# Seven half-size products in one line, read from a shifted x

## The chip, the cores and the metric

The kernel runs on one core of one Trainium2 chip. The metric is the device time of one execution in microseconds (us). Three runs of the kernel before stand beside one profiled execution, from which all other times are taken.

## The reference

One sequence of 512 tokens with 1024 features passes two layers. Layer 0 mixes by a gated delta rule (six heads, chunked) beside a cross-attention into 256 memory tokens; layer 1 by sliding-window attention (12 query heads on a shared K/V, window 128, sinks) beside the same kind of cross-attention. Each mixer and each MLP is followed by `h = layer_norm(alpha * h + y)`. What the change concerns is the MLP, once in each layer:

```python
def sq_relu_mlp(h, w_up, w_down):            # w_up (1024, 4096), w_down (4096, 1024)
    return jnp.square(jax.nn.relu(h @ w_up)) @ w_down
```

All is float32.

## The kernel before, in words

**Split operands.** A float32 operand is kept as two tiles, a high part (h, hi, H) and the rest (l, lo, L). A product is three matmuls for each block of 128 features: high by high, high by low, low by high. The high part is made by a cast on ScalarE (ACT), the rest by a subtraction on VectorE (DVE): `wload` (L87, L88) for weights used as loaded, `split_copy` (L118, L119) elsewhere. The features of all tokens lie in XH and XL, [128, 8, 512] each.

**The MLP (`mlp`, L775).** The 4096 hidden features are eight chunks of 512. The first chunk (`ups_first`, 256 tokens at a time) and half of the second (`ups_second`) are made by plain products. All others go in pairs of 128-feature groups, two pairs to a chunk, by a Strassen-like scheme: for a pair, the 2 x 2 blocks (two groups, two halves of the tokens, two halves of the 1024 features) need seven half-size products instead of eight. `x_sums` (L831) makes three combinations of the blocks of x once in a layer (TH and TL, T2 to T4). `up_load` (L852) loads a pair's weights and makes four combinations on GpSimd (POOL), sa and sb; `Pair.split0`, `split_b`, `split_a` and `split2` make high and low parts of raw[0], sb, sa and half of raw[1] (w2h, w2l).

A product (`product`, L863) is twelve matmuls of 256 columns: four feature blocks, three matmuls each. The seven are

- m1 (A11 on x's block B11), into PSUM tile a; ACT copies it to s1. m2 (A12 on B21) adds onto a; ACT takes the relu of it into r.
- m6 (S2 on T2), into PSUM tile b; DVE makes u2 = s1 + b. m7 (S3 on T3) adds onto b; DVE makes u3 = s1 + b (L915) and, from it and d, a quarter of r (L916). m4 (A22 on T4) adds onto b again; DVE makes another quarter (L924).
- m5 (S1 on T1), into PSUM tile d. m3 (S4 on B22) adds onto d; DVE makes the last quarter (L928).

`close` (L930) squares r and splits it into hh and hl of the chunk being made ("later").

**The order.** The loop of L972 goes over seven chunks c and two halves n of the output features. One step is: the products m1, m6, m2, m5 and m7 of a pair of chunk c + 1; the first down tile of chunk c (`down`, L936: twelve matmuls of 512 columns for 128 tokens, added to the residual res by DVE); m4; the second down tile; m3 and `close`; the third and the fourth down tile. Between these calls stand the loads and splits of the down weights (`dn_slabs`) and of the next pair (`Pair`, `split0`, `split_b`, `split_a`). The first step of a layer has `ups_second` in place of a pair. A step with a pair is called a line in what follows.

The order in each engine's queue is fixed when the program is built. A scheduler places an instruction when its model finds its inputs ready, so the order may differ from that of the source: the cast of the next pair's first weights stands right behind m2's last use of the same buffer, two products ahead of where the source has it. Where an instruction of TensorE (PE) wasn't ready in the model, others were put ahead of it.

Weights are double: `wh` and `wl` have five buffers each, two for the down weights of a step and three for the splits of the next pair. Loads go through one queue (SP) into four buffers `wr`.

**Placement.** Pools lay their tiles one behind the other in the order of the first request for each tag, each tile rounded up to 32 bytes. In the program the start addresses within a partition, modulo 256 bytes, are: XH, XL and res 128; TH, TL, w2h and w2l 160; in the MLPs and in layer 1 wh and wl, and hh and hl, 224. Layer 1's attention features (mixh, mixl) are at 160. Blocks and halves within these tiles are 256 bytes or a multiple of it apart, so every slice that a product reads has its tile's value.

Of the kernel before, what the change touches and what calls it, by code (L numbers as in the profile page):

```python
# [11 lines left out]
F32 = mybir.dt.float32  # L12
F32R = mybir.dt.float32r
I32 = mybir.dt.int32
AF = mybir.ActivationFunctionType
ALU = mybir.AluOpType
AX = mybir.AxisListType

P = 128
S = 512  # L20
D = 1024
NT = S // P
# [27 lines left out]
def trunk(ctx: ExitStack, tc: tile.TileContext, xT, xn, memT, wk, wq, wv, wqm, wz, wmk, wmv, wo0, wo1, up, dn,  # L50
          bw, ws, conv, alog, dtb, nw, sinks, lng, lnb, lngb, pos, invf, out):
    nc = tc.nc
    V, G, A, T, SY = nc.vector, nc.gpsimd, nc.scalar, nc.tensor, nc.sync
# [8 lines left out]
    def nm(s):  # L62
        uid[0] += 1
        return f"{s}_{uid[0]}"

    def ct(shape, tag, dt=F32):
        return cp.tile(shape, dt, tag=tag, name=tag)

    def mmt(n="mm"):
        return pmm.tile([P, 512], F32, tag="mm", name=nm(n))  # L70
# [4 lines left out]
    def fr(ap):  # L75
        return ap.bitcast(F32)
# [4 lines left out]
    def wload(src, shape):  # L81
        wp = wpool[0]
        raw = wp.tile(shape, F32, tag="wr", name=nm("wr"), bufs=wpool[1])
        SY.dma_start(raw, src)
        hi = wp.tile(shape, F32R, tag="wh", name=nm("wh"), bufs=wpool[2])
        lo = wp.tile(shape, F32R, tag="wl", name=nm("wl"), bufs=wpool[2])
        A.copy(hi, raw)  # L87
        V.tensor_sub(lo, raw, fr(hi))  # L88
        return hi, lo

    XH = ct([P, KT, S], "XH", F32R)
    XL = ct([P, KT, S], "XL", F32R)
    res = ct([P, NT, D], "res")
    lns = ctx.enter_context(tc.tile_pool(name="lns", bufs=2))
    wa_stack = ExitStack()
    wpool[0] = wa_stack.enter_context(tc.tile_pool(name="wa", bufs=3))
# [20 lines left out]
    def split_copy(src, hi, lo):  # L117
        A.copy(hi, src)  # L118
        V.tensor_sub(lo, src, fr(hi))  # L119
# [8 lines left out]
    def tok(t):  # L128
        return slice(t * P, (t + 1) * P)
# [11 lines left out]
    def c0(shape, tag, dt=F32):  # L141

        return km0.tile(shape, dt, tag=tag, name=tag)
# [3 lines left out]
    ones = c0([P, P], "ones")  # L147
# [1 line left out]
    triu = c0([P, P], "triu")  # L149
    G.affine_select(triu, ones, [[1, P]], ALU.is_ge, 0.0, base=0, channel_multiplier=-1)  # L150
    slow = c0([P, P], "slow", F32R)
    slow32 = c0([P, P], "slow32")
    G.affine_select(slow32, ones, [[-1, P]], ALU.is_gt, 0.0, base=0, channel_multiplier=1)
    V.tensor_copy(slow, slow32)
    mtri = c0([P, P], "mtri")
    G.memset(mtri, 0.0)
    G.affine_select(mtri, mtri, [[1, P]], ALU.is_ge, NEG, base=0, channel_multiplier=-1)
    band = ct([P, 256], "band")
# [8 lines left out]
    convw = ct([P, 18, 4], "convw")  # L167
    gbT = ct([P, 4, 2, KT], "gbT")

    def row_bcast(src, n, tag):  # L170
        t = ct([P, n], tag)
        SY.dma_start(t, src.rearrange("(o n) -> o n", o=1).broadcast_to([P, n]))
        return t

# [22 lines left out]
    for i in range(2):  # L197
# [5 lines left out]
        for m in range(2):  # L203
            ps = mmt("VM")
            token_major(ps[:, :256], slabs, lambda k: MH[:, m, k, :], lambda k: ML[:, m, k, :])
            A.copy(VM[i][:, m, :], ps[:, :256])
        for j in range(2):
            w = wload(wmk[i, j], [P, KT, P])
            ps = mmt("KM")
            feature_major(ps[:, :256], w, lambda k: MH[:, :, k, :], lambda k: ML[:, :, k, :])  # L210
            A.copy(KM[i][:, j, :], ps[:, :256])
    for t in range(NT):
        split_load(xT[t], XH[:, :, tok(t)], XL[:, :, tok(t)])
    SY.dma_start(convw, conv)
    SY.dma_start(gbT, lngb)
    alog_b = row_bcast(alog, NH, "alog_b")
    dtb_b = row_bcast(dtb, NH, "dtb_b")
    nw_b = row_bcast(nw, P, "nw_b")
    sink_b = row_bcast(sinks, 12, "sink_b")
    invf_b = row_bcast(invf, 32, "invf_b")  # L220
    pos_i = ct([P, NT], "pos_i", I32)
# [11 lines left out]
    def proj_z(zg, gates=None):  # L233
# [4 lines left out]
        for t in range(NT):  # L238
            ps = mmt("proj_zMM")
            token_major(ps[:, :CW], slabs, x_tok(XH, t), x_tok(XL, t))  # L240
            A.copy(res[:, t, c0:c0 + n], ps[:, :n])
            if gates is not None:
                V.tensor_copy(gates[:, :, t], ps[:, n:n + 12])

    ab = ct([P, 12, NT], "ab")
    proj_z(2, ab)


    gg = [ct([P, 24], f"gate{i}") for i in range(12)]
    (ga, gb_, ge, gs, gs2, gacc, g_, beta, eg, neg, egl, gt) = gg  # L250

    def v6(t):
# [19 lines left out]
    for n in (13, 11, 9, 7, 5, 3, 1):  # L272
# [6 lines left out]
    A.activation(ea, alog_b, AF.Exp)  # L279
    V.scalar_tensor_tensor(v6(g_), v6(ga), -1.0, ea[:, :].unsqueeze(2).broadcast_to([P, NH, NT]),  # L280
                           op0=ALU.mult, op1=ALU.mult)
    gsp = [ct([P, 24], f"gsplit{i}", F32R) for i in range(2)]
    split_copy(g_, *gsp)
    ps = smt("v6ps")
    T.matmul(ps[:, 0:24], triu, g_, start=True, stop=True)
# [42 lines left out]
    def group_kq(gi, hl):  # L328
# [5 lines left out]
        for which, (wsrc, chb) in enumerate(((wk, 6), (wq, 0))):  # L334
            ps = mmt("kq")
            feature_major(ps, wload(wsrc[h], [P, KT, P]), x_all(XH), x_all(XL))
            conv_silu(ps, chb + h, kq[:, hl, :, which, :])
# [33 lines left out]
    def group_v(gi, hl):  # L371
        g = groups[gi]
        h = GH * gi + hl
        ps = mmt("v")
        feature_major(ps, wload(wv[h], [P, KT, P]), x_all(XH), x_all(XL))
        g["vt", hl] = dt_([P, 4, P], "vt")
# [221 lines left out]
    def features_half(src, t, j):  # L598

        pt = smt("to_feapt").rearrange("p (a i) -> p a i", a=4)  # L600
        for a in range(4):
            T.transpose(pt[:, a, :], src[:, (4 * j + a) * P:(4 * j + a + 1) * P], ident)
        hs, ls = XH[:, 4 * j:4 * j + 4, tok(t)], XL[:, 4 * j:4 * j + 4, tok(t)]
        A.copy(hs, pt)
# [14 lines left out]
    def proj_qm(j):  # L619
        ps = mmt("qm")  # L620
        feature_major(ps, wload(wqm[j], [P, KT, P]), x_all(XH), x_all(XL))
        A.copy(res[:, :, 768 + j * P:768 + (j + 1) * P], ps.rearrange("p (t i) -> p t i", t=NT))
# [152 lines left out]
    def mlp(pool, layer, last, gb0):  # L775
        NC = 8
        HT = 256
        kA, kB = slice(0, 4), slice(4, 8)
        tA, tB = slice(0, HT), slice(HT, S)
# [17 lines left out]
        def new_hid():  # L797
            return hid_tiles(F32R)
# [30 lines left out]
        xq = {}  # L829

        def x_sums():  # L831
            q = lambda k, t: (XH[:, k, t], XL[:, k, t])
            x11, x12, x21, x22 = q(kA, tA), q(kA, tB), q(kB, tA), q(kB, tB)
            t1 = f4([P, 4, HT], "t1")
            if layer == 0:
                f11, f12, f21, f22 = (xf[j][:, :, t] for j in range(2) for t in (tA, tB))
            else:
                f11, f12, f21, f22 = t1, *(f4([P, 4, HT], n) for n in ("f12", "f21", "f22"))
                for f, x in ((f11, x11), (f12, x12), (f22, x22), (f21, x21)):
                    V.tensor_tensor(f, fr(x[0]), fr(x[1]), op=ALU.add)  # L840
            V.tensor_sub(t1, f12, f11)
            V.tensor_sub(f12, f22, f12)
            V.tensor_sub(f22, f22, t1)
            V.tensor_sub(f21, f21, f22)
            TH, TL = (pool.tile([P, 3, 4, HT], F32R, tag=n, name=nm(n), bufs=1) for n in ("TH", "TL"))
            for i, t in enumerate((f22, f12, f21)):
                split_copy(t, TH[:, i], TL[:, i])

            xq.update(t1=t1, B11=x11, B21=x21, B22=x22, T1=x12,
                      **{n: (TH[:, i], TL[:, i]) for i, n in enumerate(("T2", "T3", "T4"))})  # L850
# [9 lines left out]
            G.tensor_tensor(sb[:, 1], raw[0][:, kB], sb[:, 0], op=ALU.subtract)  # L860
            return raw, sa, sb

        def product(ps, w, x, start, stop):  # L863
            (hi, lo), (mh, ml) = w, x
            for k in range(4):
                T.matmul(ps, hi[:, k, :], mh[:, k, :], start=start and k == 0, stop=False, skip_group_check=True)  # L866
                T.matmul(ps, hi[:, k, :], ml[:, k, :], start=False, stop=False, skip_group_check=True)  # L867
                T.matmul(ps, lo[:, k, :], mh[:, k, :], start=False, stop=stop and k == 3, skip_group_check=True)  # L868

        class Pair:  # L870
# [23 lines left out]

            def m1(self):
                self.a = smt("upa")[:, 0:HT]
                product(self.a, self.A11, xq["B11"], True, False)
                self.s1 = self.small("m1")
                A.copy(self.s1, self.a)

# [11 lines left out]
            def m7(self):  # L912
                product(self.b, self.S3, xq["T3"], False, False)
                self.u3 = self.small("u3")
                V.tensor_tensor(self.u3, self.s1, self.b, op=ALU.add)  # L915
                V.tensor_tensor(self.r[:, 1, tB], self.u3, self.d, op=ALU.add)  # L916

            def m5(self):
                self.d = smt("upd")[:, 0:HT]
                product(self.d, self.S1, xq["T1"], True, False)  # L920

            def m4(self):
                product(self.b, self.A22, xq["T4"], False, True)
# [48 lines left out]
        for c in range(NC - 1):  # L972
            later = new_hid()
            for n in range(2):
                p, nxt = nxt, None
                first = c == 0 and n == 0
                f0 = 4 * c + 2 * n + 6
                if first:
                    ups_second(later)
                    slabs = dn_slabs(c, n)  # L980
                else:
                    p.m1()
                    p.m6()
                    p.split2()
                    slabs = dn_slabs(c, n)
                    p.m2()
                    p.m5()
                    p.m7()
                if layer == 0 and c == 0:
                    ln_affine(gb0, ALPHA, n)  # L990
                if f0 < 4 * NC:
                    nxt = Pair(f0)
                down(c, 0, n, hid, slabs)
                if not first:
                    p.m4()
                if nxt:
                    nxt.split0()
                down(c, 1, n, hid, slabs)
                if not first:
                    p.m3()  # L1000
                    p.close(later)
                if nxt:
                    nxt.split_b()
                down(c, 2, n, hid, slabs)
                if nxt:
                    nxt.split_a()
                down(c, 3, n, hid, slabs)
            if c == 0:
                gb1 = load_gb(2 * layer + 1)
            if c == 2 and layer == 0:  # L1010
                rotary_tables(pool)
            hid = later
# [262 lines left out]
```

## Time and profile before

| | |
|---|---|
| runs | 1190.02, 1191.41, 1192.32 us; median 1191.41 |
| profiled execution | 1191.65 us, of it span 1189.9 us |
| mean granted clock of TensorE | 0.991 |
| PE matmuls | 7512, busy 1158.1 us |
| PE weight loads | busy 1025.7 us |
| VectorE / ScalarE / GpSimd | busy 866.3 / 566.3 / 229.0 us |
| DMA | 114.17 MB, 96 GB/s over the span |

In rows of the timeline the first column is the start in us from the span's start, the second the duration, then the engine, the line of the kernel, the operation, what it writes and reads (`out<-in`, buffer numbers left out), its shapes and how many were merged. In brackets stands the idle time before it on its engine and what ended that. PEld is a weight load of PE, POOL is GpSimd. Records of matmuls overlap, since one begins to stream before the results of the one before have landed: the pace of PE is the difference of two starts, not the duration.

### The profile page before, as it was taken

What the parts mean: (1) busy time and instruction counts of PE and PEld (TensorE: products, weight loads), DVE (VectorE), ACT (ScalarE), POOL (GpSimd) and SP (SyncE); (2) the same over time, 40 slices, a digit from 0 to 9 for tenths busy, and PEclk for the clock granted to TensorE, in tenths of its full rate; (3) what the DMA queues carried; (4) which work ended last, traced back from release to release, by engine and by line L of the source; (5) the groups of instructions that cost most, each with busy time, mean ns of one, the idle gap of its engine ahead of it and who ended that gap; (6) DMA issues with size and microseconds to landing.
All of it is one profiled execution on the core that took longest, in us unless ns stands there. A gap on an engine that the chain in (4) does not pass through costs nothing.

```text
span 1189.9 us, 19072 instructions
## 1 busy us (share of the span) xinstructions
PE 1158.1 (97%) x7512; PEld 1025.7 (86%) x7512; DVE 866.3 (73%) x1621; ACT 566.3 (48%) x1024; POOL 229.0 (19%) x180
## 2 busy tenths in 40 slices
PE   9899999999999999999999999999999999999996
PEld 8877788879998898998988888788989998989985
DVE  5478889777798666666656968886986666666657
ACT  5345454655484443545443346662653534445341
POOL 0112111101014413232220100000042314232204
PEclk9899999999999999999999999999999999999998
DMA  7522141204324232232424231112333242323311
GB/s 255 176 72 78 60 132 39 67 19 139 130 82 139 79 121 93 90 123 71 141 73 124 72 120 41 38 35 71 107 112 119 74 139 72 128 86 101 112 36 71
DMA packets 41242, 114.17 MB, mean 96 GB/s; under 512 B 12160, under 2 KB 12544, under 8 KB 41152
## 3 DMA queue, kind: packets, MB, share of 16 engines
q1 hardware_dynamic: 40576, 112.04, 28.9%
q8 instruction: 59, 0.97, 0.3%
q10 hardware_dynamic: 576, 0.92, 0.2%
q14 instruction: 31, 0.25, 0.1%
HBM read 109.53 MB, written 3.41 MB: 95 GB/s over the span
## 4 chain that ended last, share of the span: by engine, by line
PE 81%; DVE 11%; ACT 3%; DMA 1%; POOL 1%; issue 1%; POOLq 0%; SPq 0%; ACTq 0%; DVEq 0%
PE dn L113 9%; PE dn L114 9%; PE dn L112 9%; PE upb L866 3%; PE upb L867 3%; PE upb L868 3%; PE wo L113 2%; PE wo L114 2%; PE wo L112 2%; PE upa L867 2%; PE upd L867 2%; PE upa L868 2%; PE upd L868 2%; PE upa L866 2%; PE upd L866 2%; PE up L103 2%
## 5 line engine op out<-in xcount | busy, mean ns | idle before, releaser
L114 PE MATMUL dn<-wh,hl 128*128 128x512 f32 x512 | 200.0, 391 | 0.0
L113 PE MATMUL dn<-wl,hh 128*128 128x512 f32 x512 | 200.0, 391 | 0.0
L112 PE MATMUL dn<-wh,hh 128*128 128x512 f32 x512 | 199.6, 390 | 0.0
L87 ACT CAST wh<-wr 128x1024 fp32r<-128x1024 f32 (+1 forms) x136 | 142.5, 1051 | 103.8 <-PE dn L114 24.8
L88 DVE TENSOR_TENSOR wl<-wr,wh 128x1024 fp32r<-128x1024 f32 (+1 forms) x136 | 166.4, 1225 | 34.1 <-ACT wh L87 31.7
L114 PEld LDWEIGHTS dn<-wh,hl 128*128 128x128 f32 x512 | 96.1, 188 | 20.3
L945 DVE TENSOR_TENSOR res<-res,dn 128x512 f32<-128x512 f32 x120 | 82.0, 683 | 40.7 <-PE dn L114 40.2
L112 PEld LDWEIGHTS dn<-wh,hh 128*128 128x128 f32 x512 | 96.4, 188 | 17.6
L113 PEld LDWEIGHTS dn<-wl,hh 128*128 128x128 f32 x512 | 96.1, 188 | 17.7
L857 POOL TENSOR_TENSOR sa<-wr 128x512 f32<-128x512 f32 x26 | 36.1, 1388 | 370.6 <-DMA wr<-in_up_dram 279.6
L651 POOL TENSOR_TENSOR rs<-rs,nhalf 128x1 f32<-128x1 f32 x16 | 13.3, 834 | 338.1 <-DVE rs L650 282.0
L119 DVE TENSOR_TENSOR wl<-wr,wh 128x1024 fp32r<-128x1024 f32 x26 | 34.1, 1310 | 43.5 <-ACT wh L118 43.5
L118 ACT CAST wh<-sa 128x1024 fp32r<-128x1024 f32 x26 | 27.3, 1050 | 76.6 <-PE upd L867 76.6
L867 PE MATMUL upa<-XL,wh 128*128 128x256 f32 x208 | 58.5, 281 | 0.0
L867 PE MATMUL upd<-XL,wh 128*128 128x256 f32 x208 | 58.5, 281 | 0.0
L868 PE MATMUL upa<-XH,wl 128*128 128x256 f32 x208 | 58.4, 281 | 0.0
L868 PE MATMUL upd<-XH,wl 128*128 128x256 f32 x208 | 58.3, 280 | 0.0
L866 PE MATMUL upa<-XH,wh 128*128 128x256 f32 x208 | 58.3, 280 | 0.0
L866 PE MATMUL upd<-XH,wh 128*128 128x256 f32 x208 | 58.2, 280 | 0.0
L866 PE MATMUL upb<-TH,wh 128*128 128x256 f32 x208 | 58.0, 279 | 0.0
L867 PE MATMUL upb<-TL,wh 128*128 128x256 f32 x208 | 57.8, 278 | 0.0
L868 PE MATMUL upb<-TH,wl 128*128 128x256 f32 x208 | 57.6, 277 | 0.0
(411 smaller groups left out, 3365.7 us busy)
## 6 DMA issues: line engine op xcount, KB each, us to landing
wr<-in_up_dram SPq DMA_DIRECT2D x64, 512.0 KB, 5.4
wr<-in_dn_dram SPq DMA_DIRECT2D x64, 512.0 KB, 4.6
wr<-in_wo_dram SPq DMA_DIRECT2D x16, 512.0 KB, 3.8
wr<-in_bw_dram SPq DMA_DIRECT2D x8, 512.0 KB, 4.3
wr<-in_wz_dram SPq DMA_DIRECT2D x6, 520.0 KB, 4.5
wr<-in_wk_dram SPq DMA_DIRECT2D x6, 512.0 KB, 3.7
wr<-in_wq_dram SPq DMA_DIRECT2D x6, 512.0 KB, 3.5
wr<-in_wv_dram SPq DMA_DIRECT2D x6, 512.0 KB, 3.7
```

Of the source, the lines that this page charges most:

```text
L87: A.copy(hi, raw)
L88: V.tensor_sub(lo, raw, fr(hi))
L112: T.matmul(ps, sh, hi[:, kk, :], start=(k == 0), stop=False)
L113: T.matmul(ps, sh, lo[:, kk, :], start=False, stop=False)
L114: T.matmul(ps, sl, hi[:, kk, :], start=False, stop=(k == nk - 1))
L118: A.copy(hi, src)
L119: V.tensor_sub(lo, src, fr(hi))
L857: G.tensor_tensor(sa[:, 0], raw[1][:, kA], raw[1][:, kB], op=ALU.add)
L866: T.matmul(ps, hi[:, k, :], mh[:, k, :], start=start and k == 0, stop=False, skip_group_check=True)
L867: T.matmul(ps, hi[:, k, :], ml[:, k, :], start=False, stop=False, skip_group_check=True)
L868: T.matmul(ps, lo[:, k, :], mh[:, k, :], start=False, stop=stop and k == 3, skip_group_check=True)
L945: V.tensor_tensor(dst, dst, ps, op=ALU.add)
```

## The change

Three things change in the MLP. The seven products of a pair are called one after the other (m1, m6, m2, m7, m5, m4, m3), then `close`; the four down tiles follow without anything of the pair between them. m7 comes ahead of m5, and the quarter of r made from u3 and d moves from m7 to m5. And m1's first matmul of the twelve reads its moving block from a copy of it, made by ACT once in a layer.

The placement changes with it. 32 bytes ahead of XH put XH, XL and res at 160 modulo 256; 224 bytes behind res bring what follows back to where it was modulo 256. In the MLP's pool 64 and 160 bytes ahead of the copy put it at 128, 32 bytes before x's own 160, and 96 bytes behind it bring w2h and w2l to 224. For room, a mask's own tile (slow32) is dropped, its values going through mtri first, and small tiles of layer 0 (ab, the gates, gsplit, nw_b, 2048 bytes together) go to the pool that is closed with layer 0's mixer. No matmul is added or removed.

```diff
+    ct([P, 8], "pad0")
     XH = ct([P, KT, S], "XH", F32R)
     XL = ct([P, KT, S], "XL", F32R)
     res = ct([P, NT, D], "res")
+    ct([P, 56], "pad1")
...
-    slow32 = c0([P, P], "slow32")
-    G.affine_select(slow32, ones, [[-1, P]], ALU.is_gt, 0.0, base=0, channel_multiplier=1)
-    V.tensor_copy(slow, slow32)
     mtri = c0([P, P], "mtri")
+    G.affine_select(mtri, ones, [[-1, P]], ALU.is_gt, 0.0, base=0, channel_multiplier=1)
+    V.tensor_copy(slow, mtri)
     G.memset(mtri, 0.0)
...
-    ab = ct([P, 12, NT], "ab")
+    ab = c0([P, 12, NT], "ab")
...
             TH, TL = (pool.tile([P, 3, 4, HT], F32R, tag=n, name=nm(n), bufs=1) for n in ("TH", "TL"))
+            pool.tile([P, 16], F32, tag="pad2", name=nm("pad2"), bufs=1)
             for i, t in enumerate((f22, f12, f21)):
                 split_copy(t, TH[:, i], TL[:, i])
+
+            pool.tile([P, 40], F32, tag="pad3", name=nm("pad3"), bufs=1)
+            xq["first"] = pool.tile([P, HT], F32R, tag="x0", name=nm("x0"), bufs=1)
+            pool.tile([P, 24], F32, tag="pad4", name=nm("pad4"), bufs=1)
+            A.copy(xq["first"], fr(XH[:, 0, tA]))
...
-        def product(ps, w, x, start, stop):
+        def product(ps, w, x, start, stop, first=None):
             (hi, lo), (mh, ml) = w, x
             for k in range(4):
-                T.matmul(ps, hi[:, k, :], mh[:, k, :], start=start and k == 0, stop=False, skip_group_check=True)
+                m = mh[:, k, :] if k or first is None else first
+                T.matmul(ps, hi[:, k, :], m, start=start and k == 0, stop=False, skip_group_check=True)
                 T.matmul(ps, hi[:, k, :], ml[:, k, :], start=False, stop=False, skip_group_check=True)
                 T.matmul(ps, lo[:, k, :], mh[:, k, :], start=False, stop=stop and k == 3, skip_group_check=True)
...
-                product(self.a, self.A11, xq["B11"], True, False)
+                product(self.a, self.A11, xq["B11"], True, False, xq["first"])
...
                 V.tensor_tensor(self.u3, self.s1, self.b, op=ALU.add)
-                V.tensor_tensor(self.r[:, 1, tB], self.u3, self.d, op=ALU.add)
 
             def m5(self):
                 self.d = smt("upd")[:, 0:HT]
                 product(self.d, self.S1, xq["T1"], True, False)
+                V.tensor_tensor(self.r[:, 1, tB], self.u3, self.d, op=ALU.add)
...
                     p.m2()
+                    p.m7()
                     p.m5()
-                    p.m7()
+                    p.m4()
+                    p.m3()
+                    p.close(later)
...
                 down(c, 0, n, hid, slabs)
-                if not first:
-                    p.m4()
                 if nxt:
                     nxt.split0()
                 down(c, 1, n, hid, slabs)
-                if not first:
-                    p.m3()
-                    p.close(later)
```

More of the change, by code (lines that the diff above doesn't have):

```diff
@@ L168, in trunk, with row_bcast @@
     gbT = ct([P, 4, 2, KT], "gbT")
-    def row_bcast(src, n, tag):
-        t = ct([P, n], tag)
+    def row_bcast(src, n, tag, where=ct):
+        t = where([P, n], tag)
         SY.dma_start(t, src.rearrange("(o n) -> o n", o=1).broadcast_to([P, n]))
@@ L217, in trunk @@
     dtb_b = row_bcast(dtb, NH, "dtb_b")
-    nw_b = row_bcast(nw, P, "nw_b")
+    nw_b = row_bcast(nw, P, "nw_b", c0)
     sink_b = row_bcast(sinks, 12, "sink_b")
@@ L243, in proj_z @@
                 V.tensor_copy(gates[:, :, t], ps[:, n:n + 12])
-    ab = ct([P, 12, NT], "ab")
+    ab = c0([P, 12, NT], "ab")
     proj_z(2, ab)
-    gg = [ct([P, 24], f"gate{i}") for i in range(12)]
+    gg = [c0([P, 24], f"gate{i}") for i in range(12)]
     (ga, gb_, ge, gs, gs2, gacc, g_, beta, eg, neg, egl, gt) = gg
@@ L281, in trunk @@
                            op0=ALU.mult, op1=ALU.mult)
-    gsp = [ct([P, 24], f"gsplit{i}", F32R) for i in range(2)]
+    gsp = [c0([P, 24], f"gsplit{i}", F32R) for i in range(2)]
     split_copy(g_, *gsp)
```

## The prediction

> **What bounds the kernel now.** I read the page's busy times and chain first, then the timeline of TensorE (PE) over one step of an MLP, then ScalarE (ACT) and VectorE (DVE) over the same step.
>
> ```profile
> span 1189.9 us, 19072 instructions
> PE 1158.1 (97%) x7512; PEld 1025.7 (86%) x7512; DVE 866.3 (73%) x1621; ACT 566.3 (48%) x1024; POOL 229.0 (19%) x180
> PE 81%; DVE 11%; ACT 3%; DMA 1%; POOL 1%; issue 1%; POOLq 0%; SPq 0%; ACTq 0%; DVEq 0%
> ```
>
> PE is busy for 97% of the span and carries 81% of the chain. So a change pays only if it makes PE's instructions follow each other more closely, and it costs when PE has to wait. The span is 1189.9 us, the profiled execution 1191.65 us, and the median of the runs shown 1191.41 us, 0.24 us lower. I sum against 1191.65. About 0.2% (2.4 us) is what a measurement of this kernel can tell from no change.
>
> The next rows are the first matmuls of each product in one step (a "line" below): start in us, duration, operation. Only the starts matter, since matmuls overlap.
>
> ```profile
> 480.53 0.28 PE L866 MATMUL upa<-XH,wh 128*128 128x256 f32 x1
> ...
> 481.95 0.28 PE L866 MATMUL upb<-TH,wh 128*128 128x256 f32 x1
> ...
> 482.19 0.28 PE L868 MATMUL upb<-TH,wl 128*128 128x256 f32 x1
> ...
> 483.33 0.28 PE L866 MATMUL upa<-XH,wh 128*128 128x256 f32 x1
> ...
> 484.50 0.28 PE L867 MATMUL upa<-XL,wh 128*128 128x256 f32 x1
> ...
> 484.74 0.28 PE L866 MATMUL upd<-XH,wh 128*128 128x256 f32 x1
> ...
> 486.14 0.28 PE L866 MATMUL upb<-TH,wh 128*128 128x256 f32 x1
> ...
> 486.85 0.28 PE L866 MATMUL upb<-TH,wh 128*128 128x256 f32 x1
> ...
> 487.53 0.39 PE L112 MATMUL dn<-wh,hh 128*128 128x512 f32 x1
> ...
> 490.27 0.28 PE L866 MATMUL upb<-TH,w2h 128*128 128x256 f32 x1
> ...
> 491.70 0.39 PE L112 MATMUL dn<-wh,hh 128*128 128x512 f32 x1
> ...
> 494.46 0.28 PE L866 MATMUL upd<-XH,wh 128*128 128x256 f32 x1
> ...
> 495.89 0.39 PE L112 MATMUL dn<-wh,hh 128*128 128x512 f32 x1
> ...
> 498.62 0.39 PE L112 MATMUL dn<-wh,hh 128*128 128x512 f32 x1
> ...
> 501.34 0.28 PE L866 MATMUL upa<-XH,wh 128*128 128x256 f32 x1
> ...
> 503.01 0.28 PE L868 MATMUL upb<-TH,wl 128*128 128x256 f32 x1
> ...
> 504.14 0.28 PE L866 MATMUL upa<-XH,wh 128*128 128x256 f32 x1
> ```
>
> A line takes 501.34 - 480.53 = 20.81 us. Every product is twelve matmuls of one shape, yet they take, by differences of starts: m1 1.42, m6 1.38, m2 1.41, m5 1.40, m7 1.39, m4 (on w2h) 1.43 and m3 1.43, 9.86 us together; the four down tiles 2.74, 2.76, 2.73 and 2.72, 10.95 us. PE waits for nobody in there: the difference is pace. m6's last ten matmuls take 1.14 us (482.19 to 483.33) and, a line later, 1.13 (503.01 to 504.14): 113.5 ns each. m7 begins at 0.71/6 = 118 ns (486.14 to 486.85) and ends at 0.68/6 = 113.5. m1, m4 and m3 stay at 119.
>
> With the placements of the section on the kernel before, the 113.5 ns belong to a moving tile at 160 and weights at 224 (modulo 256 bytes), once something at 128 has been read just before; m1, m2, m5 and m3 move a tile at 128 over weights at 224, and m4 a tile at 160 over weights at 160, after a down tile. That is what the change builds on: it puts every operand of the seven products where m6 has them.
>
> **Part one, the line.** There are 13 lines in a layer (seven chunks with two halves, less the first), 26 in all. After the change the line is 84 matmuls on a moving tile at 160 and weights at 224, the first reading its copy at 128, as m6 is entered from m1. I take 113.5 ns: 84 x 0.1135 = 9.53 us, and 0.03 us for settling (m7's first six at 118 ns instead of 113.5). The down tiles are entered once instead of three times: 2.74 + 3 x 2.72 = 10.90. The line is then 20.46 us, 0.35 us less, and 26 of them 9.1 us less. From the other side, if the pace were that of m1 and m3 (1.43), the products would take 10.01 us and the line would be 0.10 us longer: +2.6 us.
>
> The rows say that the pace of one shape depends on what it reads. The Trainium skill, "TensorE: Matmul & The Clock Gate", section "Back-to-back issue gap", gives the gap at full clock as N/2.4 + 2.5 ns, which depends on the width alone (109 ns for 256, 216 for 512); by it this part, and the next but one, would be worth nothing. The trace disagrees: 113.5 and 119 ns stand side by side at one width.
>
> **Part two, a wait that the new order brings.** m7's sum leaves PSUM through u3 (L915), and m4 adds onto the same PSUM tile, so m4's first weight load must wait for u3. Now a down tile (2.74 us) lies between; afterwards only m5 does (1.36 us).
>
> ```profile
> 484.82 1.05 ACT L118 CAST wh<-wr 128x1024 fp32r<-128x1024 f32 x1 [2.29 <-PE upa L867]
> 485.90 1.22 DVE L119 TENSOR_TENSOR wl<-wr,wh 128x1024 fp32r<-128x1024 f32 x1 [1.88 <-ACT wh L118]
> 487.73 0.42 DVE L915 TENSOR_TENSOR u<-m,upb 128x256 f32<-128x256 f32 x1 [0.61 <-PE upb L868]
> ```
>
> As soon as m2's eleventh matmul (484.50) has given up the weights, ACT casts the next pair's into their buffer, and DVE takes the rest (wl) before u3. Counted from m2's end (484.74): cast at +0.08, wl from +1.16 to +2.38. u3's input will now be there one product and 0.20 us (487.53 to 487.73) after m2's end, at +1.56, while wl has held DVE since +1.16. So u3 runs from about +2.42 to +2.84, and m4 would be due at 2 x 1.362 = +2.72. That wl stays ahead of u3 in DVE's fixed order I take from a like case: at the end of the line wl of the down weights stands before the sum of the last down tile, though they are ready almost together (that tile's matmuls gave way to m1 at 480.53).
>
> ```profile
> 480.46 1.22 DVE L88 TENSOR_TENSOR wl<-wr,wh 128x1024 fp32r<-128x1024 f32 x1
> 481.60 0.68 DVE L945 TENSOR_TENSOR res<-res,dn 128x512 f32<-128x512 f32 x1
> ```
>
> What a wait for DVE costs beyond the delay:
>
> ```profile
> 777.11 0.68 DVE L119 TENSOR_TENSOR pTl<-spt,pTh 128x512 fp32r<-128x512 f32 x1
> ...
> 777.85 0.42 PEld L1145 LDWEIGHTS spt<-ident,pm 128*128 128x128 f32 x4 [0.56 <-DVE pTl L119]
> ```
>
> ```profile
> 682.19 0.19 PEld L112 LDWEIGHTS ropeMM<-wh,XH 128*128 128x128 f32 x1 [0.76 <-ACT vSh L118]
> ...
> 682.22 0.36 PE L112 MATMUL ropeMM<-wh,XH 128*128 128x256 f32 x1 [0.58 <-DVE rp L1043]
> ...
> 682.42 0.28 PE L113 MATMUL ropeMM<-wl,XH 128*128 128x256 f32 x1
> ```
>
> The weight load starts 0.06 us after DVE's end (777.79), the matmul 0.03 later, and the second matmul follows after 0.20 instead of 0.12 us. So m4 starts at +2.93, 0.21 late, and with 0.08 for the restart the wait costs 0.29 us. Behind it on PE's queue stand m4, m3 and all four down tiles: nothing hides it. It is paid where a next pair is cast, 12 lines of a layer, 24 in all: +7.0 us. The bounds are 0 (u3 goes first, or other matmuls fill the gap) and 0.29; I take 0.29, since its rows are of this very place. r's quarter (L916), which goes from m7 to m5, follows u3 at once and is ready long before m3 rewrites its tile.
>
> **Part three, other readers of x.** ups_first reads XH and XL as moving tiles over weights at 224, now at 128:
>
> ```profile
> 345.20 0.28 PE L103 MATMUL up<-XL,wh 128*128 128x256 f32 x1
> ...
> 354.33 0.39 PE L102 MATMUL up<-XH,wh 128*128 128x512 f32 x1
> ...
> 365.58 0.39 PE L112 MATMUL dn<-wh,hh 128*128 128x512 f32 x1
> ```
>
> From 345.20 to 354.33 there are 77 matmuls of 256 columns, 118.6 ns each; then 48 of 512 in 11.25 us, 234.4 ns each. With x at 160 the first become m6's case: 2 layers x 192 x (118.6 - 113.5) = 2.0 us less. No copy leads them in, so 0 is the other bound. For 512 columns at 160 over 224 there is no row; between no change and the down tiles' 2.72/12 = 226.7 ns (0.7 us over 96 matmuls) I take half, 0.4 us.
>
> In the projections x is the stationary side:
>
> ```profile
> 699.81 0.39 PE L112 MATMUL projqMM<-wh,XH 128*128 128x512 f32 x1
> ...
> 704.24 0.39 PE L113 MATMUL projqMM<-wl,XH 128*128 128x512 f32 x1
> ```
>
> 19 matmuls in 4.43 us, 233.2 ns. With x elsewhere they may fall to 226.7 or rise to 240 (twice the slowest 256-wide pace, 1.43/12 = 119, and a little): over the 288 such matmuls of layer 1, 1.9 us less or more. Layer 0's projections, on weights of several placements, I bound alike. I take 0 for these and keep 3 us either way for the range.
>
> **Parts that cost nothing.** The copy is one ACT instruction per layer, well before the first line, on an engine 48% busy. POOL's fill of mtri now waits for DVE's copy out of it, at the start, and nothing early reads what stands behind it on POOL. Tiles moved to the other pool keep their instructions. m4's and m3's sums reach DVE and ACT 2.7 to 7 us earlier than now, out of the down tiles' time; the hidden tile they make is first read a whole line later. SP's queue keeps its order of loads, and the sums on POOL wait for those as before.
>
> **Sum.** 1191.65 - 9.1 + 7.0 - 2.0 - 0.4 = 1187.2 us.
>
> **The rivals.**
>
> *The wait is covered (chance 0.31).* The pace comes as above, but u3 is done in time: it is put ahead of wl, or matmuls of the first down tile are put in front of m4. For it: where one operation wasn't ready, PE's order has others in between, as here a projection between transposes.
>
> ```profile
> 713.96 0.33 PE L1145 MATMUL spt<-ident,pm 128*128 128x128 f32 x1
> 714.04 0.48 PE L112 MATMUL projqMM<-wh,XH 128*128 128x512 f32 x1
> 714.36 0.93 PE L1145 MATMUL spt<-ident,pm 128*128 128x128 f32 x7
> ```
>
> One down matmul (0.227 us) would cover nearly all of it. Against it: in today's lines PE's order is that of the source, and the gap is so short that it may not have been seen when the order was made. Time: 1187.2 - 7.0 = 1180.2 us.
>
> *The pace is lost at the wait (0.16).* m4 and m3 restart without a copy leading them in and run as m4 and m3 do now, 1.43 instead of 1.36: 0.14 us x 26 = 3.5 us more, 1190.7 us.
>
> *Slower: the pace does not follow the placement (0.14).* What m6 has may come from the twelve matmuls at 128 before it, not from one; m7, entered alike, needed six matmuls to settle. Then the products keep their 9.86 us, the readers of part three gain nothing, only the down tiles' 0.05 us x 26 = 1.3 us remain, and the wait is paid: 1191.65 + 7.0 - 1.3 = 1197.4 us. It decides from a gain per line under 7.0/26 = 0.27 us, a mean pace above 114.4 ns (9.53 + 0.35 - 0.27 = 9.61 us over 84). The skill's rule on the gap, quoted above, has no term for placement and points the same way.
>
> **How the numbers follow.** My forecast, gain and wait together, gets 0.39. With 3 us of uncertainty from part three around it, about a quarter of it falls within 0.2%. The covered wait lies wholly on the fast side, the lost pace mostly within 0.2%, the last rival wholly on the slow side. Faster: 0.29 + 0.31 + 0.03 = 0.63; within: 0.09 + 0.11 = 0.20; slower: 0.01 + 0.02 + 0.14 = 0.17. The range goes from the covered wait less 2.7 us, 1177.5, to the lost pace and 3.3 us, 1194.0; the last rival is left out.
>
> **What would show it.** In the timeline of PE the 84 matmuls of a line should lie 113.5 ns apart from the second or third on, and a line should take about 20.75 us with the wait and 20.46 without. u3 behind wl and an idle weight load of m4 released by DVE would show the wait; a down matmul between m5 and m4 would show it covered. ups_first should go from 118.6 to 113.5 ns. It is wrong if m2 or m5 keep 117 ns, if m4 starts without a wait in unchanged order, or if projections change by more than 3 us.

## The result

| | before | after |
|---|---|---|
| median of four runs | 1191.87 us | 1185.35 us |
| lowest and highest | 1190.02 and 1192.34 | 1184.96 and 1185.52 |
| profiled execution, its span | 1191.65, 1189.9 us | 1185.52, 1183.8 us |
| mean granted clock of TensorE | 0.991 | 0.992 |

The ratio of the times is 0.9948, 95% interval 0.993 to 0.9965: the changed kernel is faster by 6.5 us, and its time lies 1.9 us below the forecast of 1187.2. These are the lines of the page after that answer to those of before:

```profile
span 1183.8 us, 19079 instructions
PE 1148.7 (97%) x7512; PEld 1017.0 (86%) x7512; DVE 864.5 (73%) x1621; ACT 563.4 (48%) x1026; POOL 247.9 (21%) x180
PE 82%; DVE 12%; ACT 3%; POOL 1%; issue 1%; DMA 1%; POOLq 0%; SPq 0%; ACTq 0%; DVEq 0%
```

PE still carries the chain, with the same 7512 matmuls, and is busy for 9.4 us less. One line of layer 0 in the timeline of PE, the first matmul of each product and of the down tiles (L875 to L877 are now what L866 to L868 were, L115 what L112 was):

```profile
498.99 0.28 PE L875 MATMUL upa<-x,wh 128*128 128x256 f32 x1
...
500.37 0.28 PE L875 MATMUL upb<-TH,wh 128*128 128x256 f32 x1
...
501.73 0.28 PE L875 MATMUL upa<-XH,wh 128*128 128x256 f32 x1
...
503.09 0.28 PE L875 MATMUL upb<-TH,wh 128*128 128x256 f32 x1
...
504.45 0.28 PE L875 MATMUL upd<-XH,wh 128*128 128x256 f32 x1
...
505.87 0.38 PE L875 MATMUL upb<-TH,w2h 128*128 128x256 f32 x1
...
507.34 0.28 PE L875 MATMUL upd<-XH,wh 128*128 128x256 f32 x1
...
508.70 0.39 PE L115 MATMUL dn<-wh,hh 128*128 128x512 f32 x1
...
519.60 0.28 PE L875 MATMUL upa<-x,wh 128*128 128x256 f32 x1
```

By differences of starts: m1 1.38, m6 1.36, m2 1.36, m7 1.36, m5 1.42, m4 1.47, m3 1.36, the four down tiles 10.90, the line 20.61 us where it was 20.81. Four products run at 1.36/12 = 113.3 ns a matmul; m1 takes 0.02 us longer to reach that pace. What m5 and m4 have above it is the wait for u3, at the end of the one and the start of the other.

Summed from the starts in the two traces, the 26 lines with their waits gained 3.6 us: 2.6 in layer 1, only 1.0 in layer 0. ups_first gained 0.9, the 512-wide matmuls behind it 0.1. The remaining 1.5 us lie outside the MLPs. Most of that is the start of the program, where the first matmul into kq comes 2.51 us earlier than before, and some is given back later. Here is that matmul, in the timeline before:

```profile
56.66 0.39 PE L102 MATMUL kq<-XH,wh 128*128 128x512 f32 x1
```

and after:

```profile
54.15 0.39 PE L105 MATMUL kq<-XH,wh 128*128 128x512 f32 x1
```

**What layer 0 lost.** In the first line of layer 0, m7 stands still (timeline after, several engines):

```profile
377.73 0.28 PE L877 MATMUL upa<-XH,wl 128*128 128x256 f32 x1
377.87 1.21 DVE L88 TENSOR_TENSOR wl<-wr,wh 128x1024 fp32r<-128x1024 f32 x1
...
379.00 0.41 DVE L914 TENSOR_TENSOR u<-m,upb 128x256 f32<-128x256 f32 x1
...
379.46 0.19 PEld L875 LDWEIGHTS upb<-TH,wh 128*128 128x128 f32 x1 [1.66 <-DVE u L914]
379.47 0.38 PE L875 MATMUL upb<-TH,wh 128*128 128x256 f32 x1 [1.46 <-DVE u L914]
```

DVE is behind with the splits of the down weights (wl, L88) and the residual sums of the first step, so u2 is finished at 379.41. m7 adds onto the PSUM tile that u2 reads, and m7 now stands directly behind m2, where m5 used to lie between. It starts 379.47 - 377.73 = 1.74 us after m2's last matmul instead of 0.11: 1.63 us, once in the program. Its second matmul follows 0.22 us later instead of 0.11, so the stall costs 1.7 us in all.

### The profile page after: what moved, and what is told of

Read it like the earlier page. It is cut to its first block, busy times and chain, and to the rows that moved or that the text cites. A ratio compares the mean times of both kernels' runs of the same rounds, so it can differ in the third digit from the quotient of the medians.

```text
span 1183.8 us, 19079 instructions
## 1 busy us (share of the span) xinstructions
PE 1148.7 (97%) x7512; PEld 1017.0 (86%) x7512; DVE 864.5 (73%) x1621; ACT 563.4 (48%) x1026; POOL 247.9 (21%) x180
## 4 chain that ended last, share of the span: by engine, by line
PE 82%; DVE 12%; ACT 3%; POOL 1%; issue 1%; DMA 1%; POOLq 0%; SPq 0%; ACTq 0%; DVEq 0%
PE dn L116 9%; PE dn L117 9%; PE dn L115 9%; PE upb L875 3%; PE upb L877 3%; PE upb L876 3%; PE wo L116 2%; PE wo L117 2%; PE wo L115 2%; PE upa L876 2%; PE upa L875 2%; PE upa L877 2%; PE upd L876 2%; PE upd L877 2%; PE upd L875 2%; PE up L106 2%
## 5 line engine op out<-in xcount | busy, mean ns | idle before, releaser
L88 DVE TENSOR_TENSOR wl<-wr,wh 128x1024 fp32r<-128x1024 f32 (+1 forms) x136 | 166.6, 1226 | 79.6 <-ACT wh L87 79.1
L115 PE MATMUL dn<-wh,hh 128*128 128x512 f32 x512 | 199.5, 390 | 0.0
L865 POOL TENSOR_TENSOR sa<-wr 128x512 f32<-128x512 f32 x26 | 44.2, 1702 | 349.0 <-DMA wr<-in_up_dram 294.8
L115 PEld LDWEIGHTS dn<-wh,hh 128*128 128x128 f32 x512 | 96.1, 188 | 19.0
L875 PE MATMUL upb<-TH,wh 128*128 128x256 f32 x208 | 57.5, 277 | 1.5 <-DVE u L914 1.5
L877 PE MATMUL upa<-XH,wl 128*128 128x256 f32 x208 | 57.5, 276 | 0.0
L877 PE MATMUL upb<-TH,wl 128*128 128x256 f32 x208 | 57.4, 276 | 0.0
L875 PE MATMUL upd<-XH,wh 128*128 128x256 f32 x208 | 57.4, 276 | 0.0
L877 PE MATMUL upd<-XH,wl 128*128 128x256 f32 x208 | 57.4, 276 | 0.0
L866 POOL TENSOR_TENSOR sb<-sa,wr 128x512 f32<-128x512 f32 x26 | 57.4, 2207 | 0.0
L121 ACT CAST wh<-wr 128x1024 fp32r<-128x1024 f32 x26 | 27.4, 1055 | 53.6 <-PE upa L876 53.6
```

Of the source, the lines that this page charges most:

```text
L115: T.matmul(ps, sh, hi[:, kk, :], start=(k == 0), stop=False)
L865: G.tensor_tensor(sa[:, 0], raw[1][:, kA], raw[1][:, kB], op=ALU.add)
L866: G.tensor_tensor(sb[:, 0], sa[:, 0], raw[0][:, kA], op=ALU.subtract)
L875: T.matmul(ps, hi[:, k, :], m, start=start and k == 0, stop=False, skip_group_check=True)
```

## The experiments

The kernels were timed on several occasions, so each has its ratio to the kernel before on the same chip, and the verdicts rest on the traces rather than on a microsecond of time. A handy sign there: in the view of groups by line the mean recorded length of a 256-column matmul goes with its pace, 281 ns where they follow each other every 117.7 ns, 276 where every 113.3. Three such groups before (columns: line, operation, count, busy us, mean ns, idle before):

```profile
L867 PE MATMUL upa<-XL,wh 128*128 128x256 f32 x208 | 58.5, 281 | 0.0
...
L868 PE MATMUL upd<-XH,wl 128*128 128x256 f32 x208 | 58.3, 280 | 0.0
...
L867 PE MATMUL upb<-TL,w2h 128*128 128x256 f32 x104 | 29.4, 283 | 0.0
```

and after:

```profile
L876 PE MATMUL upa<-XL,wh 128*128 128x256 f32 x208 | 57.7, 277 | 0.0
...
L877 PE MATMUL upd<-XH,wl 128*128 128x256 f32 x208 | 57.4, 276 | 0.0
...
L876 PE MATMUL upb<-TL,w2h 128*128 128x256 f32 x104 | 28.8, 276 | 0.0
```

"upa" is m1 and m2, "upd" m5 and m3, the rows on w2h are m4.

Two theories of the pace stand against each other. By the first it belongs to the placement: a matmul whose operands lie at 160 and 224 runs fast, whatever came before. By the second it belongs to the history: it is set where a run of matmuls begins, by a first read at 128 followed by reads at 160. A rival to both is that the gain comes from the new order.

### The copy left out (no_copy)

```
-                product(self.a, self.A11, xq["B11"], True, False, xq["first"])
+                product(self.a, self.A11, xq["B11"], True, False)
```

> The changed kernel, but m1's first matmul reads x's own block at 160 instead of the copy at 128 (the copy is still made). Theory P (placement alone draws the pace): a moving tile at 160 over weights at 224 settles at 113.5 ns whatever was read before, so a line grows by 0.03 us at most and the time stays within 1 us of the changed kernel's 1185.35. Theory H (entry): the pace is set by what is read when the line is entered, and then kept; coming from down tiles at 224 straight to 160 the products run at 117 to 120 ns like m4 before the change, 84 x 26 x 3.5 to 6.5 ns = 8 to 14 us more: 1193 to 1199.

1187.68 us (12 runs), ratio 0.9983 [0.9971, 0.9995]. The groups of this kernel:

```profile
L876 PE MATMUL upa<-XL,wh 128*128 128x256 f32 x208 | 58.4, 281 | 0.0
...
L877 PE MATMUL upd<-XH,wl 128*128 128x256 f32 x208 | 58.0, 279 | 0.0
```

One changed read in 84 slows m1, and then m6, m2, m7 and m5 with it, all to 1.41 us. So the pace is not each matmul's own, since m6's operands are untouched: it is handed on, and the placement theory falls. But upd stands between 276 and 281, because m3 runs at 1.36 in most lines: behind m4's wait the pace is fast again. The loss is smaller than the expectation's larger number, as the slow pace is 117.7 ns and not 119 to 120, and as the wait ends it.

### x back at 128, its copy at 96 (x_128)

```
-    ct([P, 8], "pad0")
-    ct([P, 56], "pad1")
-            pool.tile([P, 40], F32, tag="pad3", name=nm("pad3"), bufs=1)
+            pool.tile([P, 32], F32, tag="pad3", name=nm("pad3"), bufs=1)
-            pool.tile([P, 24], F32, tag="pad4", name=nm("pad4"), bufs=1)
+            pool.tile([P, 32], F32, tag="pad4", name=nm("pad4"), bufs=1)
```

> The changed kernel with x back at 128 modulo 256 and the copy 32 bytes before it, at 96; order and all else as changed. If placement sets the pace (P, and H as well, since x and TH then alternate between 128 and 160), m1, m2, m5 and m3 go back to 117 to 119 ns: 48 x 26 x 4 to 5.5 ns = 5 to 7 us more, and ups_first and the projections give back about 1 to 3 us: 1191 to 1195. If the one line alone had brought the gain, the time stays at 1185.4.

1191.18 us (11 runs), ratio 1.0007 [0.9997, 1.0017]. Groups of this kernel (its lines are two lower):

```profile
L875 PE MATMUL upd<-XH,wl 128*128 128x256 f32 x208 | 58.5, 281 | 0.0
L875 PE MATMUL upa<-XH,wl 128*128 128x256 f32 x208 | 58.3, 281 | 0.0
```

The new order and a copy 32 bytes below x, but with x at 128: no gain at all. In its timeline the first matmuls of m6, m2, m7 and m5 are

```profile
498.92 0.28 PE L873 MATMUL upb<-TH,wh 128*128 128x256 f32 x1
...
500.29 0.28 PE L873 MATMUL upa<-XH,wh 128*128 128x256 f32 x1
...
501.70 0.28 PE L873 MATMUL upb<-TH,wh 128*128 128x256 f32 x1
...
503.11 0.28 PE L873 MATMUL upd<-XH,wh 128*128 128x256 f32 x1
```

Here m6 alone, a step from 128 to 160, gets down to 1.37 us, and m2 behind it, back at 128, loses it again. But m7 behind m2 is the same step, and stays at 1.41. So a read at 128 ahead of reads at 160 doesn't always bring the fast pace; what else it takes, no run shows.

### The copy at other places (copy_160, copy_192)

In copy_160:

```
-            pool.tile([P, 40], F32, tag="pad3", name=nm("pad3"), bufs=1)
+            pool.tile([P, 48], F32, tag="pad3", name=nm("pad3"), bufs=1)
-            pool.tile([P, 24], F32, tag="pad4", name=nm("pad4"), bufs=1)
+            pool.tile([P, 16], F32, tag="pad4", name=nm("pad4"), bufs=1)
```

> The copy of x's first block is kept, but lies at 160 modulo 256, as x itself does. Theory one (a line's first reads at 128, followed by reads at 160, put TensorE at the fast pace): this copy is then as good as none, m1, m6, m2, m7 and m5 take 1.41 us, a line 20.76, the time is that of the kernel without the copy, about 1187.7 us. Theory two (any block at an address of its own does it, since the second matmul then no longer reads x beside the same place): 1.36 us a product, 1185.4 us.

1188.86 us (10 runs), ratio 0.9984 [0.9969, 0.9998]. In copy_192 the two sizes are 56 and 8.

> The copy lies at 192 modulo 256, 32 bytes above x and no longer 32 below. Theory one (it takes a read at 128 before 160): as without the copy, products of 1.41 us, about 1187.7 us. Theory two (any first block 32 bytes off does it): products of 1.36 us, 1185.4 us. [...]

1187.73 us (10 runs), ratio 0.9979 [0.9963, 0.9995]. The group of upa is in both kernels, line for line, the one shown for no_copy, and so is that of upd in copy_160. In copy_192 it is

```profile
L877 PE MATMUL upd<-XH,wl 128*128 128x256 f32 x208 | 57.9, 278 | 0.0
```

Both kernels are as without the copy. A copy is not enough, nor is one 32 bytes away: of the places tried, only 128 ahead of 160 does it.

### m4 in a PSUM tile of its own (m4_own)

```
-                product(self.b, self.S3, xq["T3"], False, False)
+                product(self.b, self.S3, xq["T3"], False, True)
...
-                product(self.b, self.A22, xq["T4"], False, True)
-                V.tensor_tensor(self.r[:, 1, tA], self.s1, self.b, op=ALU.add)
+                e = smt("upe")[:, 0:HT]
+                product(e, self.A22, xq["T4"], True, True)
+                V.tensor_tensor(self.r[:, 1, tA], self.u3, e, op=ALU.add)
```

> The changed kernel with m4 in a PSUM tile of its own (the quarter of r is then u3 plus that tile), so m4 no longer waits for u3. If the wait costs what the trace of the changed kernel shows, 0.18 us in 24 lines, the time is 1185.35 - 4.3 = 1181.0, a line 20.43 us, and m7's single wait of 1.6 us in layer 0's first line stays. Rival: m3 then waits for r's quarter on d instead, or the new tile is late, and nothing is gained: 1185.4.

1179.31 us (4 runs), ratio 0.9915 [0.99, 0.9929]. The same place of a line in this kernel's timeline:

```profile
505.43 0.41 DVE L924 TENSOR_TENSOR u<-m,upb 128x256 f32<-128x256 f32 x1
505.72 0.28 PE L877 MATMUL upd<-XH,wl 128*128 128x256 f32 x1
505.73 0.19 PEld L875 LDWEIGHTS upe<-TH,w2h 128*128 128x128 f32 x1
505.83 0.28 PE L875 MATMUL upe<-TH,w2h 128*128 128x256 f32 x1
```

u3 runs as late as in the changed kernel, to 505.84, but m4 loads at 505.73 and starts at 505.83, 0.11 us behind m5's last matmul. All seven products take 1.36 to 1.38 us and the line 20.43, in all lines but layer 0's first, where m7's stall remains. That is 0.18 us under the changed kernel's mean of 20.616 in layer 1: the whole price of the wait, by itself.

### Neither copy nor wait (no_copy_m4_own)

The edits of no_copy and m4_own together.

> Neither the lead-in copy nor the wait for u3: m1 starts on x's own block, and m4 has a PSUM tile of its own. Theory (the pace is set where a run of matmuls begins and kept until PE waits): nothing resets the line after its start, so all seven products take 1.41 us, m4 and m3 too, a line 20.80 us, 26 x 0.36 us more than the same kernel with the copy (1179.3 us): 1188.8 us. Rival (m4 and m3 are fast by their own placement, the wait has nothing to do with it): m4 and m3 at 1.36 us, a line 20.70 us, 1186.2 us.

1188.11 us (10 runs), ratio 0.9982 [0.9969, 0.9996]. Groups of this kernel:

```profile
L877 PE MATMUL upd<-XH,wl 128*128 128x256 f32 x208 | 58.4, 281 | 0.0
...
L876 PE MATMUL upe<-TL,w2h 128*128 128x256 f32 x104 | 29.2, 281 | 0.0
```

Now m4 and m3 are slow too: all seven products of a layer 1 line take 1.41, the line 20.77 us. With the copy the same instructions on the same operands take 20.43. So one read in 84 sets the pace of the other 83, as long as nothing stops PE. m3 was 1.36 in 69 of the 75 lines of no_copy, copy_160 and copy_192 in which m4 waits (all but a layer 0 line, the first), and in none of those 25 here. The wait is what changes the pace there, but not always. After m7's stall in the first line the pace was fast in three of these four kernels and slow in one. It can go the other way too: in m4_own, with the copy, the pace was fast up to the stall, and m5, m4 and m3 behind it took 1.41.

### The old order on the new placement (old_order)

```
                     p.m2()
-                    p.m7()
                     p.m5()
-                    p.m4()
-                    p.m3()
-                    p.close(later)
+                    p.m7()
...
                 down(c, 0, n, hid, slabs)
+                if not first:
+                    p.m4()
...
                 down(c, 1, n, hid, slabs)
+                if not first:
+                    p.m3()
+                    p.close(later)
```

The quarter of r made from u3 and d goes back into m7.

> The new placement and the copy for m1, but the old order: m1, m6, m2, m5, m7, a down tile, m4, a down tile, m3, so m4 and m3 are entered from down tiles without a copy. m4's wait for u3 (0.18 us in 24 lines, 4.3 us) and the single wait of 1.6 us of m7 for u2 in layer 0's first line go; the down tiles are entered three times again (+1.3 us). Theory P: m4 and m3 keep 113.5 ns, 1185.35 - 4.3 - 1.6 + 1.3 = 1180.8. Theory H: m4 and m3 run at 119, 0.14 x 26 = 3.6 us more: 1184.4.

1180.47 us (6 runs, 1176.58 to 1183.74), ratio 0.9927 [0.9909, 0.9944]. All six lie under the changed kernel's four, though the intervals of the two ratios touch. Groups of this kernel:

```profile
L877 PE MATMUL upd<-XH,wl 128*128 128x256 f32 x208 | 57.9, 278 | 0.0
...
L876 PE MATMUL upb<-TL,w2h 128*128 128x256 f32 x104 | 29.2, 281 | 0.0
```

m4 and m3, entered from a down tile, take 1.41 each, the five behind the copy 1.36 to 1.38, the line 20.54. There is no wait for u3, and of m7's stall in layer 0 0.26 us is left. The time is near the expectation's lower number, but not for its reason: m4 and m3 are slow, as the higher supposes, only at 1.41 and not 1.43 (1.0 us in 26 lines), and the four down tiles take 10.90 us although they are entered three times, so the 1.3 us counted for that didn't come. Corrected by both, the higher number is 1182.1; the profiled execution took 1182.82, and the six runs spread around 1180.47. Twelve lines of each layer take 246.9 and 246.5 us here, 249.0 and 247.4 in the changed kernel. So putting the seven products in one line costs more in waits than it gains in pace: 3 us of a total that the placement and the copy made.

### The old order with a second copy, for m4 (old_lead4)

To old_order's edits come a tile behind xq["first"], also at 128, with a copy of T4's first block, and

```
-                product(self.b, self.A22, xq["T4"], False, True)
+                product(self.b, self.A22, xq["T4"], False, True, xq["first4"])
```

> The order of the kernel before (m4 and m3 behind down tiles, at 1.41 us each), with a second copied block, at 128 modulo 256, that m4 alone starts on. Theory one: m4 falls from 1.41 to 1.38 us or less, m3 stays at 1.41: 26 x 0.03 to 0.05 us = about 1 us under the same order without it (1180.5 us then): 1179.4 us. Rival (the copy works only after the wait at a line's start, not behind a stream of down matmuls): both stay at 1.41 us, 1180.5 us.

1179.55 us (4 runs), ratio 0.9917 [0.9895, 0.9939]. The group of m4 in this kernel (its lines are two higher):

```profile
L878 PE MATMUL upb<-TL,w2h 128*128 128x256 f32 x104 | 29.0, 278 | 0.0
```

In the timeline m4 falls from 1.41 to 1.38 us and m3 stays at 1.41: a copy works behind a stream of down matmuls too. But the down tile that follows m4 takes 2.74 instead of 2.72, so the line gets only 0.02 us shorter, 20.52 in layer 1. The time can't tell that from old_order.

### m4's own tile, m5 ahead of m7 (m4_own_m5_first)

To m4_own's edits, m5 is called ahead of m7 and the quarter of r goes back into m7.

> m4 in a PSUM tile of its own (no wait for u3), and m5 ahead of m7, with r's quarter on the other side of it in m7. Theory: the one-off stall of 1.5 us in layer 0's first line, m7 waiting for u2, goes, since m5 lies in between; all else is as in the kernel with m4's own tile: 1179.3 - 1.6 = 1177.7 us, lines 20.43 us in both layers. Rival: m3 now waits for r's quarter to have read d, and the line gets a wait of 0.1 to 0.2 us: 1180 to 1183 us.

1178.19 us (4 runs, 1176.07 to 1181.47), ratio 0.9903 [0.9876, 0.9931]. In layer 0's first line (timeline):

```profile
376.36 0.28 PE L877 MATMUL upd<-XH,wl 128*128 128x256 f32 x1
...
376.78 0.19 PEld L875 LDWEIGHTS upb<-TH,wh 128*128 128x128 f32 x1 [0.34 <-DVE u L914]
```

The stall of 1.6 us is down to 376.78 - 376.36 - 0.11 = 0.3, lines take 20.43 us in layer 1, and m3 waits for nothing. Twelve lines of layer 0 take 245.6 us from first to last start, against 247.1 in m4_own: 1.3 of these 1.5 us are the shorter stall, the rest is the slow pace behind it in m4_own. The runs of the two overlap, so the trace shows this gain and the times do not: two runs at a mean granted clock of 0.995 took 1176.07 and 1176.47 us, the two at 0.989 and 0.990 took 1181.47 and 1179.92. Its median is the lowest of all versions, but its interval overlaps those of m4_own and old_lead4.

## Why the prediction was right, and where it was off

The forecast case happened: the line with its copy runs at the fast pace, and m4 waits for u3. Its single terms:

**Part one (line pace, -9.1 us): right.** m4_own's line, 20.43 us, is the predicted 20.46 without the wait, and the down tiles take the predicted 10.90. At 26 x (20.81 - 20.43) = 9.9 us the term was 0.8 short. The reason given for it held for the line: without the first read at 128 (no_copy) it is slow. As a rule it fails in two places: m7 of x_128 reads at 160 over weights at 224 right behind reads at 128 and takes 1.41, and m3 of no_copy takes 1.36 behind the wait with no read at 128. What the weights' place at 224 adds no run tests, since the weights of the products lie there in every version of the changed kernel. The rival with the slower result, that the pace doesn't follow the placement, is dead for this order; x_128 shows what it would have looked like. The formula that the prediction quotes from the Trainium skill ("TensorE: Matmul & The Clock Gate", section "Back-to-back issue gap") depends on the width alone: 109 ns for all kernels here. The section gives it for an isolated matmul, and for a stream of weight loads and matmuls, which this kernel is, about 131 ns at 512 columns; the prediction leaves that out, and the down tiles here take 226.7. The runs have 113.3 and 117.7 on the same instructions of 256 columns, and the whole gain of the lines lies in that difference.

**Part two (the wait, +7.0 us): the mechanism right, the size too large.** The rows of the wait after:

```profile
503.17 1.06 ACT L121 CAST wh<-wr 128x1024 fp32r<-128x1024 f32 x1 [2.23 <-PE upa L876]
...
504.26 1.23 DVE L122 TENSOR_TENSOR wl<-wr,wh 128x1024 fp32r<-128x1024 f32 x1 [1.84 <-ACT wh L121]
...
505.40 0.41 DVE L924 TENSOR_TENSOR u<-m,upb 128x256 f32<-128x256 f32 x1
505.69 0.28 PE L877 MATMUL upd<-XH,wl 128*128 128x256 f32 x1
...
505.87 0.19 PEld L875 LDWEIGHTS upb<-TH,w2h 128*128 128x128 f32 x1
505.87 0.38 PE L875 MATMUL upb<-TH,w2h 128*128 128x256 f32 x1
...
506.09 0.28 PE L876 MATMUL upb<-TL,w2h 128*128 128x256 f32 x1
```

Cast, wl, u3 and then m4's idle load stand in the order foreseen. From m2's end (503.09) u3 runs from +2.31 to +2.72, not +2.42 to +2.84: it is recorded as starting before wl's record ends (504.26 + 1.23 = 505.49). Two DVE records in a row overlap by 0.09 us here, and the row that the prediction itself took for DVE's order shows as much (480.46 + 1.22 = 481.68, the next at 481.60). The sum counted the durations one after the other. And m4's first matmul starts with its load, not 0.03 later. So m4 is 505.87 - 505.69 - 0.11 = 0.07 us late instead of 0.21, and its second matmul follows after 0.22 instead of 0.11, the restart: 0.18 us in all, not 0.29. It is paid in 25 lines, one more than forecast: not in layer 0's first, but also in the last of each layer, which the prediction left out. That is 4.5 us.

**Not in the sum: the one-off stall of 1.7 us.** The prediction worked out one wait, from a line in the middle of a layer. That m7 had moved up to m2 as well, and u2 in the first line is late, it didn't look at. A row of DVE in that line of the kernel before would have shown it:

```profile
381.07 0.41 DVE L905 TENSOR_TENSOR u<-m,upb 128x256 f32<-128x256 f32 x1
```

There u2 ends at 381.48, 0.8 us after m2, behind which m5 starts at 380.67.

**The rival of the covered wait** did not come: PE's order is the source's. **The rival of the pace lost at the wait** went the other way round: m3 behind the wait takes 1.36, and in the kernels without a working copy the wait even brings the fast pace.

**Part three (ups_first -2.0, 512-wide -0.4): mis-sized.** They gave 0.9 and 0.1. In ups_first, starts of matmuls 48 apart, first in layer 0, then twice in layer 1, on both sides of the transposes (L604) that stand in this stage (timeline after):

```profile
345.30 0.28 PE L106 MATMUL up<-XL,wh 128*128 128x256 f32 x1
...
350.74 0.28 PE L106 MATMUL up<-XL,wh 128*128 128x256 f32 x1
...
838.53 0.28 PE L106 MATMUL up<-XL,wh 128*128 128x256 f32 x1
...
843.97 0.28 PE L106 MATMUL up<-XL,wh 128*128 128x256 f32 x1
...
844.61 0.63 PE L604 MATMUL to_feapt<-ident,res 128*128 128x128 f32 x4
...
848.80 0.28 PE L106 MATMUL up<-XL,wh 128*128 128x256 f32 x1
...
854.45 0.28 PE L106 MATMUL up<-XL,wh 128*128 128x256 f32 x1
```

5.44/48 = 113.3 ns in layer 0 and in layer 1 ahead of the transposes, the expected pace; behind them 5.65/48 = 117.7, the slow one, with the same operands. In the eight other profiles with x at 160, no_copy among them, both layers have 113.3 to 114.0 there; with x at 128 (before and x_128) 117.7 to 118.8. So the term holds for the placement, and the restart behind the transposes brought the slow pace in this execution alone. That cost 0.6 us: layer 1's stage takes 23.77 us here and 23.19 in no_copy. Much of the rest of the shortfall lies ahead of the transposes, where the faster pace gains little: the transposes start 0.42 us after the matmul ahead of them (844.19 to 844.61), before 0.26 (847.75 to 848.01).

**Projections and the rest (0 +/- 3).** They came out at -1.5 us, within the bound. The 2.5 us at the program's start are not x's placement: in x_128, which has x at 128, kq starts at 53.70. In the other nine profiles with the small tiles moved it starts between 53.75 and 55.17. Whether the gain comes from the moved small tiles and the mask, or from the one execution of before that was profiled, stays open.

Together, against the forecast's sum: 0.8 us more gained by the pace, 2.5 less lost to the wait, 1.7 lost to the stall, 1.4 less gained in part three, 1.5 gained in the rest. That is 1.7 us below it, as the profiled execution was. The mechanism was foreseen; that the time came out so close is partly luck, since errors of up to 2.5 us cancelled.

## What to carry to other kernels

A pace that differs between equal matmuls may belong to how the run of them was entered and not to their operands: look at the first reads, and at what stands just behind a wait, before moving data. When products are put closer together, check each engine that must empty a PSUM tile in between, in the first line of a stage as well as in the middle, and add starts, not recorded durations. A sum that shares a PSUM tile can cost more than a tile: here the sharing took 4.5 us of the 9.9 that the pace had brought.

## What the runs showed of the hardware

- Two paces for one and the same instruction stream, 113.3 and 117.7 ns for 256 columns, 4% apart. The clock isn't the difference: in m4_own and in no_copy_m4_own it was granted at 1.00 from 400 to 600 us. A stretch of matmuls keeps the pace that it started in, in no_copy_m4_own and m4_own across all seven products, which change the PSUM tile six times.
- The entry that gave the fast pace behind a stream of matmuls was a read at 128 (modulo 256 bytes) followed by reads at 160; 160 then 160, 192 then 160, and 96 then 128 did not. It isn't a rule: m7 of x_128, entered by the same step from 128 to 160, stayed slow. Why the memory or the array does so no run shows.
- A hold-up of PE can change the pace. In the three kernels without a working copy m4's second matmul comes 0.17 to 0.18 us after the first instead of 0.12, and the slow pace turned fast in 69 of 75 such cases. In the changed kernel the fast pace stayed fast in all 25 lines with the wait, but it turned slow behind the transposes in layer 1's ups_first, and in m4_own behind m7's stall. So a short wait is no pure loss where the pace was slow: in no_copy m4 took 0.02 us more for it, and m3 0.05 less.
- A restart behind a wait costs more than the lateness: at m4 of the changed kernel 0.07 us late and 0.11 us for the restart.
